# Norm's factor of the up product behind the down product, and state-space parameters prepared on VectorE

## The chip, the core and the metric

The kernel runs on one core of a Trainium2 chip. The core has TensorE (matmuls into PSUM), VectorE, ScalarE, GpSimd and SyncE, which issues most DMAs; each engine has its own queue and works in order, and semaphores order the engines against each other. The metric is the device time of one execution in microseconds (us), the median of several runs.

## The reference

One decode step of a hybrid model with two layers. 272 prompt tokens (16 meta tokens and 256) go as one sequence and 8 sample tokens as eight sequences of one, so 280 columns in all, in fp32. A layer is

```
h = x + 0.5 * swiglu(rmsnorm(x))          # ffn1: 1024 -> 2816 -> 1024
proj = rmsnorm(h) @ w_in                  # 1024 -> 2304
h = h + concat(s5, rwkv7, rglru) @ w_out  # three mixers on parts of proj
h = h + 0.5 * swiglu(rmsnorm(h))          # ffn2
swiglu(x) = (silu(x @ w_gate) * (x @ w_up)) @ w_down
```

`rmsnorm` divides each token by the root of its mean square: a factor for each column, once the activations lie with features on partitions and tokens in columns. The s5 mixer has parameters of its own that depend on weights alone: for 24 groups of 64 complex states a step `ab = exp(lambda * dt)`, an input matrix `bb = ((ab - 1) / lambda) * b`, and `c`. From them come, for four tokens at once, the powers of `ab` times `bb` and times `c`, and a table of cosines and sines.

## The kernel before

**Layout.** Activations `hres` are 8 tiles of 128 features by 280 tokens. Each fp32 operand of a large matmul is split in two fp32r parts, high and low (`xh`, `xl`; for weights `whi`, `wlo`), and a product takes three matmuls (`gemm`, L200 to L202). `wpiece` (L179) fetches a weight piece of 128 x 512, copies it to `whi` on ScalarE (L191) and takes the difference `wlo` on VectorE (L192: two inputs, both in SBUF). There are five buffers for the fetched piece, five for `whi`, four for `wlo`.

**The feed-forward block** (`ffn`, L313) runs four times. It takes the norm's factor `rs` (for each column, over the constant KR) once. Then 22 tiles f: gate and up product (24 matmuls each), the gate scaled by `rs` (L335), its tanh on ScalarE (L337), the up product scaled by `rs` (L339), their product (L340), times 1 + tanh (L341), and the split into `hh` on ScalarE (L342) and `hl` on VectorE (L343). Then 8 columns j of the down product, 66 matmuls each, added into `hres` with the factor 0.25 (L354), squared into the next norm's sum, and split for the next stage.

**The work beside it.** `beside` is a generator whose steps, up to a `yield`, are put in after chosen f and j (`slots`). In two blocks it is `s5_prepare` (ffn1 of layer 0, for that layer, and ffn2 of layer 0, for layer 1), with the slots `PREP`; in the other two (ffn1 of layer 1, ffn2 of layer 1) it writes the mixers' states, with the slots `STATE`. The scheduler that places the instructions keeps to the data and to these bounds from below, and may put a step's instructions later among those of the block.

**`s5_prepare`.** States and parameters are loaded, `lru_rates` and `exp_small` compute on columns of 2 or 12 (VectorE, many small instructions); `lam_times` (L455) multiplies the entering state by `ab`; sine and cosine on ScalarE (L517, L559); the rotation table `cs` from products of 17 coarse and 4 fine angles (L570 to L572), 408 columns at a time, on GpSimd. Then complex products, `ctimes` (L576): each takes four products on GpSimd (L583, L585) and two on VectorE (L584), first 12 pairs x 16 columns for `bb`, then for each T of three (4 pairs each) three more for the powers and four with 32 columns for `ct`. Between these, a T copies the powers into `bx` (L610, ScalarE), transposes `c` (L620) and `bx` (L630) on TensorE through the one bank of `psD`, copies them out (`c0` L624 on VectorE, `xbt` L631 on ScalarE), and multiplies them into `kin` (L638, L643, L646).

Of the kernel before, what the change touches and what calls it, by code (L numbers as in the profile page):

```python
# [19 lines left out]
KD = 8  # L20
# [54 lines left out]
def tile_hybrid_decode(ctx, tc, *args):  # L75
# [237 lines left out]
    def ffn(l, which, acc, cols, gnext, beside, slots):  # L313
# [6 lines left out]
        with tc.tile_pool(name="hid", bufs=1) as hp:  # L320
# [5 lines left out]
            for f in range(FT):  # L326
# [12 lines left out]
                V.scalar_tensor_tensor(u1, pu[:, :n], KR, rs, op0=MUL, op1=MUL)  # L339
                V.tensor_tensor(g1, g1, u1, op=MUL)  # L340
# [6 lines left out]
            for j in range(KD):  # L347
                js = slice(j * P, j * P + P)
                pd = psAB()
                for a, b in ((0, 8), (8, 16), (16, 22)):  # L350
                    w = wpiece(wd[:, a:b, js])
                    gemm(pd[:, :n], w, list(range(b - a)), hh[:, :, :n], hl[:, :, :n], list(range(a, b)), a == 0,
                         b == FT)
                V.scalar_tensor_tensor(hres[:, j, cols], pd[:, :n], 0.25, hres[:, j, cols], op0=MUL, op1=ADD)  # L354
                acc_sq(j, acc2, cols)
                if gnext is not None:
                    split_x(j, gnext, cols)
                if FT + j in slots:
                    next(job, None)
# [95 lines left out]
    def lam_times(out, lar, lai, hr, hi):  # L455

        sh = [P, NPA, ND]
        w = lambda: tmp("a", 6)[:, :NPA * ND].rearrange("p (a b) -> p a b", a=NPA)
        arb, aib = lar.unsqueeze(2).to_broadcast(sh), lai.unsqueeze(2).to_broadcast(sh)
        for r, x0, x1, op in ((0, hr, hi, SUB), (1, hi, hr, ADD)):  # L460
            a, b = w(), w()
            G.tensor_tensor(a, arb, x0, op=MUL)
            G.tensor_tensor(b, aib, x1, op=MUL)
            G.tensor_tensor(out[:, r], a, b, op=op)

    def s5_prepare(l, tp, e):
# [57 lines left out]
        for r, nm in enumerate(('re_in', 'im_in')):  # L524
            G.tensor_copy(e['h0'][:, r], e[nm][:, :, 0:ND])
# [36 lines left out]
        for p0 in (0, 6):  # L562
# [6 lines left out]
            for dst, x0, x1, y0, y1, op in ((co, ca, cb, sa, sb, SUB), (sn, sa, cb, ca, sb, ADD)):  # L569
                G.tensor_tensor(dst, x0, x1, op=MUL)  # L570
                G.tensor_tensor(t4, y0, y1, op=MUL)
                G.tensor_tensor(dst, dst, t4, op=op)  # L572
            yield
        e['cos'], e['sin'] = cs[:, 0], cs[:, 1]

        def ctimes(dst, ar, ai, x, shape, conj):  # L576

            n = shape[1] * shape[2]
            w = lambda: tmp("a", 6)[:, :n].rearrange("p (a b) -> p a b", a=shape[1])
            arb, aib = ar.unsqueeze(2).to_broadcast(shape), ai.unsqueeze(2).to_broadcast(shape)  # L580
            for r, op in ((0, ADD if conj else SUB), (1, SUB if conj else ADD)):
                p0, p1 = w(), w()
# [18 lines left out]
        c0 = tp.tile([P, 2, 4, 2, 16], F32, name="c0", tag="c0")  # L601
        G.memset(c0, 0.0)
        for T in range(3):
            ts = slice(4 * T, 4 * T + 4)
            sh = [P, 4, 16]
            b = bb[:, :, ts]
            for s in range(3, -1, -1):
                for q in range(2):
                    qs = slice(64 * q, 64 * q + 64)
                    S.activation(bx[qs, :, :, s, q], b[qs], AF.Copy)  # L610
                if s:
                    nb = tp.tile([P, 2, 4, 16], F32, name="nb", tag="nb", bufs=2)
                    ctimes(ri(nb), lar[:, ts], lai[:, ts], ri(b), sh, False)
                    b = nb
            yield
            pt = psD()
            for r in range(2):
                cd = tp.tile([P, 2, 64], F32, name="cd", tag="cd", bufs=2)
                G.tensor_copy(cd, cn[:, T, r].unsqueeze(1).to_broadcast([P, 2, 64]))
                PE.transpose(pt[:, r * P:r * P + P], cd.rearrange("p q n -> p (q n)"), ident)  # L620
            pv = pt[:, :2 * P].rearrange("p (r a q c) -> p r a q c", r=2, a=4, q=2)
            for q in range(2):
                qs = slice(64 * q, 64 * q + 64)
                V.tensor_copy(c0[qs, 0, :, q], pv[qs, 0, :, q])  # L624
                V.tensor_scalar(c0[qs, 1, :, q], pv[qs, 1, :, q], -1.0, None, op0=MUL)
# [10 lines left out]
            for a in range(4):  # L636
                for r in range(2):
                    PE.matmul(pv[:, a], bx[:, r, a].rearrange("p s q c -> p (s q c)"),  # L638
                              c0[:, r, a].rearrange("p q c -> p (q c)"), start=(r == 0), stop=(r == 1))
            dd = tp.tile([P, 4, 32], F32, name="dd", tag="dd")  # L640
            G.tensor_tensor(dd[lo], ident[lo, lo].unsqueeze(1).to_broadcast([32, 4, 32]),
                            d32[lo, ts].unsqueeze(2).to_broadcast([32, 4, 32]), op=MUL)
            V.tensor_tensor(dd[lo], pv[lo], dd[lo], op=ADD)  # L643
            for d in range(4):
                for j in range(4 - d):
                    S.activation(kin[32 * j:32 * j + 32, ts, j + d], (pv if d else dd)[96 - 32 * d:128 - 32 * d],  # L646
                                 AF.Copy)

            x = [c0[:, r].rearrange("p a q c -> p a (q c)") for r in range(2)]
# [883 lines left out]
    PREP = [f for f in range(FT) if f % 3 < 2] + list(range(FT, FT + KD))  # L1533
# [61 lines left out]
```

## Time and profile before

| | |
|---|---|
| median of 3 runs | 1278.68 us (1273.01 to 1279.05) |
| the profiled execution | 1279.83 us, span 1278.0 us |
| TensorE, VectorE | 1222.5 and 999.5 us busy |
| ScalarE, GpSimd | 690.2 and 348.9 us busy |
| mean granted clock of TensorE | 0.958 |

The span is the time from the first to the last instruction of the profiled execution. The first down column of the four blocks is evicted at 176.4, 598.2, 810.9 and 1208.0 us, the last at 239.9, 658.6, 869.1 and 1262.5; the mixers lie between the first and the second block and between the third and the fourth. Matmuls are pipelined, so a busy TensorE need not go at its full pace; the number of matmuls in a stretch says that. PE is TensorE, PEld its weight loads, DVE VectorE, ACT ScalarE, POOL GpSimd, SP SyncE.

### The profile page before, as it was taken

What the parts mean: (1) busy time and instruction counts of PE and PEld (TensorE: products, weight loads), DVE (VectorE), ACT (ScalarE), POOL (GpSimd) and SP (SyncE); (2) the same over time, 40 slices, a digit from 0 to 9 for tenths busy, and PEclk for the clock granted to TensorE, in tenths of its full rate; (3) what the DMA queues carried; (4) which work ended last, traced back from release to release, by engine and by line L of the source; (5) the groups of instructions that cost most, each with busy time, mean ns of one, the idle gap of its engine ahead of it and who ended that gap; (6) DMA issues with size and microseconds to landing.
All of it is one profiled execution on the core that took longest, in us unless ns stands there. A gap on an engine that the chain in (4) does not pass through costs nothing.

```text
span 1278.0 us, 29512 instructions
## 1 busy us (share of the span) xinstructions
PE 1222.5 (96%) x10744; PEld 1161.3 (91%) x10744; DVE 999.5 (78%) x2395; ACT 690.2 (54%) x1489; POOL 348.9 (27%) x619
## 2 busy tenths in 40 slices
PE   7999899999898999989999999999999989999997
PEld 6999899988776999989998999998888779999996
DVE  7999976679687799998667878756876778987854
ACT  4556565564355555656544555556633656555552
POOL 2104852033443210385207000001615332500000
PEclk9999999989897999989999999999995989999998
DMA  7665455524311756535578665654333028866662
GB/s 187 168 182 156 132 148 154 164 83 117 92 33 50 187 160 190 156 104 169 161 185 225 194 171 167 178 168 142 105 86 93 3 83 223 237 193 177 179 187 79
DMA packets 376911, 187.49 MB, mean 147 GB/s; under 512 B 45532, under 2 KB 375352, under 8 KB 376766
## 3 DMA queue, kind: packets, MB, share of 16 engines
q1 hardware_dynamic: 376430, 184.47, 52.0%
q8 instruction: 84, 1.38, 0.4%
q10 hardware_dynamic: 336, 1.15, 0.3%
q14 instruction: 61, 0.50, 0.1%
HBM read 181.31 MB, written 3.37 MB: 145 GB/s over the span
## 4 chain that ended last, share of the span: by engine, by line
PE 79%; DVE 11%; DMA 4%; issue 2%; ACT 2%; POOL 1%; SPq 0%; DVEq 0%; ACTq 0%; POOLq 0%
PE psa L202 11%; PE psa L201 11%; PE psa L200 10%; PE psc L201 6%; PE psc L202 6%; PE psc L200 6%; PE psb L202 6%; PE psb L200 6%; PE psb L201 6%; DVE wlo L192 3%; DMA stg<-in_ffn_w_gate_dram 2%; DMA stg<-in_ffn_w_up_dram 1%; PE psc L752 1%; PE psc L677 1%; PE psc L715 1%
## 5 line engine op out<-in xcount | busy, mean ns | idle before, releaser
L191 ACT ACTIVATE whi<-stg 128x512 fp32r<-128x512 f32 (+2 forms) x664 | 399.3, 608 | 354.4 <-PE psa L201 116.1
L192 DVE TENSOR_TENSOR wlo<-stg,whi 128x512 fp32r<-128x512 f32 (+2 forms) x640 | 445.8, 700 | 129.0 <-PE psa L202 35.3
L202 PE MATMUL psa<-xh,wlo 128*128 128x280 f32 (+1 forms) x930 | 275.7, 298 | 5.0 <-DVE wlo L192 4.5
L200 PE MATMUL psa<-xh,whi 128*128 128x280 f32 (+1 forms) x930 | 273.7, 295 | 2.8 <-DVE ts L1296 2.1
L201 PE MATMUL psa<-xl,whi 128*128 128x280 f32 (+1 forms) x930 | 272.9, 294 | 0.0
L202 PEld LDWEIGHTS psa<-xh,wlo 128*128 128x128 f32 x930 | 176.4, 190 | 10.4 <-DVE wlo L192 7.9
L200 PEld LDWEIGHTS psa<-xh,whi 128*128 128x128 f32 x930 | 177.5, 191 | 5.4 <-DVE ts L1296 2.3
L201 PEld LDWEIGHTS psa<-xl,whi 128*128 128x128 f32 x930 | 177.0, 190 | 1.8 <-issue 1.0
L202 PE MATMUL psc<-xh,wlo 128*128 128x280 f32 (+1 forms) x498 | 145.1, 292 | 1.8 <-DVE wlo L192 1.8
L200 PE MATMUL psc<-xh,whi 128*128 128x280 f32 (+1 forms) x498 | 145.2, 292 | 1.0 <-ACT xh L264 0.5
L201 PE MATMUL psc<-xl,whi 128*128 128x280 f32 (+1 forms) x498 | 144.8, 291 | 1.1 <-DVE xl L265 0.7
L202 PE MATMUL psb<-xh,wlo 128*128 128x280 f32 (+1 forms) x396 | 115.6, 292 | 1.3 <-DVE wlo L192 1.3
L200 PE MATMUL psb<-xh,whi 128*128 128x280 f32 (+1 forms) x396 | 115.8, 292 | 0.2 <-ACT whi L191 0.2
L201 PE MATMUL psb<-xl,whi 128*128 128x280 f32 (+1 forms) x396 | 115.3, 291 | 0.0
L202 PEld LDWEIGHTS psc<-xh,wlo 128*128 128x128 f32 x498 | 94.0, 189 | 2.8 <-DVE wlo L192 2.7
L200 PEld LDWEIGHTS psc<-xh,whi 128*128 128x128 f32 x498 | 94.0, 189 | 2.3 <-ACT xh L738 0.8
L201 PEld LDWEIGHTS psc<-xl,whi 128*128 128x128 f32 x498 | 94.0, 189 | 1.9 <-DVE xl L265 1.0
L202 PEld LDWEIGHTS psb<-xh,wlo 128*128 128x128 f32 x396 | 74.9, 189 | 2.2 <-DVE wlo L192 2.2
L200 PE MATMUL psb<-hh,whi 128*128 128x280 f32 (+1 forms) x264 | 76.7, 291 | 0.0
L200 PE MATMUL psa<-hh,whi 128*128 128x280 f32 (+1 forms) x264 | 76.6, 290 | 0.0
L202 PE MATMUL psb<-hh,wlo 128*128 128x280 f32 (+1 forms) x264 | 76.5, 290 | 0.0
L202 PE MATMUL psa<-hh,wlo 128*128 128x280 f32 (+1 forms) x264 | 76.5, 290 | 0.0
(618 smaller groups left out, 2743.3 us busy)
## 6 DMA issues: line engine op xcount, KB each, us to landing
stg<-in_ffn_w_gate_dram SPq DMA_DIRECT2D x176, 256.0 KB
stg<-in_ffn_w_up_dram SPq DMA_DIRECT2D x176, 256.0 KB
stg<-in_ffn_w_down_dram SPq DMA_DIRECT2D x160, 256.0 KB
stg<-in_w_in_dram SPq DMA_DIRECT2D x72, 256.0 KB
stg<-in_w_out_dram SPq DMA_DIRECT2D x32, 192.0 KB
bc<-ds SPq DMA_DIRECT2D x24, 192.0 KB
stg<-in_ffn_w_down_dram SPq DMA_DIRECT2D x32, 128.0 KB
bc<-ds SPq DMA_DIRECT2D x12, 256.0 KB
```

What stands on the lines that cost most here:

```text
L191: S.activation(hi[:, :kc], st[:, :kc], AF.Copy)
L192: (eng or V).tensor_tensor(lo[:, :kc], st[:, :kc], hi[:, :kc].bitcast(F32), op=SUB)
L200: PE.matmul(out, w[wk[i]][0], ah[:, k], start=(first and i == 0), stop=False)
L201: PE.matmul(out, w[wk[i]][0], al[:, k], start=False, stop=False)
L202: im = PE.matmul(out, w[wk[i]][1], ah[:, k], start=False, stop=(last and i == n - 1))
L677: PE.matmul(px[r][:, a], s5['xbt'][:, 4 * T + a, r], u4[:, 4 * T + a, 8:16 + NQ], start=True, stop=True)
L715: PE.matmul(py[32 * i:32 * i + 32, c0:c0 + n], w, x[:, o:NQ + ND], start=(m == 0), stop=(m == 2), skip_group_check=True, tile_position=(0, ...
L752: PE.matmul(pz[:, :NT], gw[k][:, j], z5[:, k, 0:NT], start=(k == 0), stop=(k == 2))
```

## The change

Two parts. In the block, the up product is no longer scaled by the norm's factor: L339 goes, the product with the scaled gate reads the up product in PSUM, and the factor `KR * rs` is multiplied to the down product, which takes one instruction more for each j. In the preparation, the rotation, `lam_times` and the complex products go to VectorE; a complex product takes one instruction for both parts of the first factor and four for the rest, and is made for all 12 pairs at once, so there are 8 of them and not 22; copies go from GpSimd and VectorE to ScalarE; the products of `ct` come after the three T; and the work is cut into more steps, with a slot after each f from 1 to 21 and two after each j.

```
-                V.scalar_tensor_tensor(u1, pu[:, :n], KR, rs, op0=MUL, op1=MUL)
-                V.tensor_tensor(g1, g1, u1, op=MUL)
+                V.tensor_tensor(g1, pu[:, :n], g1, op=MUL)
...
-                V.scalar_tensor_tensor(hres[:, j, cols], pd[:, :n], 0.25, hres[:, j, cols], op0=MUL, op1=ADD)
+                dh = tmp("f", NRK)[:, :n]
+                V.scalar_tensor_tensor(dh, pd[:, :n], 0.25 * KR, rs, op0=MUL, op1=MUL)
+                V.tensor_tensor(hres[:, j, cols], dh, hres[:, j, cols], op=ADD)
...
-                if FT + j in slots:
+                for _ in range(slots.count(FT + j)):
                     next(job, None)
...
-            G.tensor_tensor(a, arb, x0, op=MUL)
-            G.tensor_tensor(b, aib, x1, op=MUL)
-            G.tensor_tensor(out[:, r], a, b, op=op)
+            V.tensor_tensor(a, arb, x0, op=MUL)
+            V.tensor_tensor(b, aib, x1, op=MUL)
+            V.tensor_tensor(out[:, r], a, b, op=op)
...
-            G.tensor_copy(e['h0'][:, r], e[nm][:, :, 0:ND])
+            S.activation(e['h0'][:, r], e[nm][:, :, 0:ND], AF.Copy)
...
-                G.tensor_tensor(dst, x0, x1, op=MUL)
-                G.tensor_tensor(t4, y0, y1, op=MUL)
-                G.tensor_tensor(dst, dst, t4, op=op)
+                V.tensor_tensor(dst, x0, x1, op=MUL)
+                V.tensor_tensor(t4, y0, y1, op=MUL)
+                V.tensor_tensor(dst, dst, t4, op=op)
+                yield
+        e['cos'], e['sin'] = cs[:, 0], cs[:, 1]
+
+        def ctimes(dst, ar, ai, x, n, conj, tags):
+            na = x.shape[2]
+            sh = [P, na, n]
+            p0, p1 = (tp.tile([P, 2, na, n], F32, name="cp" + tg, tag=tg) for tg in tags)
+            aib = ai.unsqueeze(2).to_broadcast(sh)
+            V.tensor_tensor(p0, ar.unsqueeze(1).unsqueeze(3).to_broadcast([P, 2, na, n]), x, op=MUL)
+            for r in range(2):
+                V.tensor_tensor(p1[:, r], aib, x[:, 1 - r], op=MUL)
             yield
-        def ctimes(dst, ar, ai, x, shape, conj):
...
-                G.tensor_tensor(p0, arb, x[r], op=MUL)
-                V.tensor_tensor(p1, aib, x[1 - r], op=MUL)
-                G.tensor_tensor(dst[r], p0, p1, op=op)
...
+            V.tensor_tensor(dst[:, 0], p0[:, 0], p1[:, 0], op=ADD if conj else SUB)
+            V.tensor_tensor(dst[:, 1], p0[:, 1], p1[:, 1], op=SUB if conj else ADD)
...
-        ctimes(ri(bb), fr, fi, ri(bn), [P, NPA, 16], False)
+        yield from ctimes(bb, fr, fi, bn, 16, False, ("sta", "stre_in"))
...
+        dd = tp.tile([P, NPA, 32], F32, name="dd", tag="dd")
+        V.tensor_tensor(dd[lo], ident[lo, lo].unsqueeze(1).to_broadcast([32, NPA, 32]),
+                        d32[lo].unsqueeze(2).to_broadcast([32, NPA, 32]), op=MUL)
+        bl = [bb]
+        for s in range(3):
+            nb = tp.tile([P, 2, NPA, 16], F32, name=f"nb{s}", tag=("ang", "nb1", "nb2")[s])
+            yield from ctimes(nb, lar, lai, bl[-1], 16, False, ("sta", "stre_in"))
+            yield
+            bl.append(nb)
...
-                    S.activation(bx[qs, :, :, s, q], b[qs], AF.Copy)
+                    S.activation(bx[qs, :, :, s, q], bl[3 - s][qs, :, ts], AF.Copy)
...
-                G.tensor_copy(cd, cn[:, T, r].unsqueeze(1).to_broadcast([P, 2, 64]))
+                S.activation(cd, cn[:, T, r].unsqueeze(1).to_broadcast([P, 2, 64]), AF.Copy)
...
-                V.tensor_copy(c0[qs, 0, :, q], pv[qs, 0, :, q])
-                V.tensor_scalar(c0[qs, 1, :, q], pv[qs, 1, :, q], -1.0, None, op0=MUL)
+                for r in range(2):
+                    S.activation(c0[qs, r, ts, 16 * q:16 * q + 16], pv[qs, r, :, q], AF.Copy, scale=-1.0 if r else 1.0)
...
-            G.tensor_tensor(dd[lo], ident[lo, lo].unsqueeze(1).to_broadcast([32, 4, 32]),
-                            d32[lo, ts].unsqueeze(2).to_broadcast([32, 4, 32]), op=MUL)
-            V.tensor_tensor(dd[lo], pv[lo], dd[lo], op=ADD)
+            V.tensor_tensor(dd[lo, ts], pv[lo], dd[lo, ts], op=ADD)
...
-            for s in range(4):
-                y = [ct[:, r, ts, s] for r in range(2)]
-                ctimes(y, lar[:, ts], lai[:, ts], x, [P, 4, 32], True)
-                x = y
-                if s & 1:
-                    yield
+            yield
+
+        x = c0
+        for s in range(4):
+            y = ct[:, :, :, s]
+            yield from ctimes(y, lar, lai, x, 32, True, ("sta", "bx"))
+            yield
+            x = y
...
-    PREP = [f for f in range(FT) if f % 3 < 2] + list(range(FT, FT + KD))
+    PREP = list(range(1, FT)) + [FT + j for j in range(KD) for _ in range(2)]
```

## Rows read from the trace of the kernel before

**Rows 1.** The page, part 1: busy us, share of the span, instructions.
```profile
PE 1222.5 (96%) x10744; PEld 1161.3 (91%) x10744; DVE 999.5 (78%) x2395; ACT 690.2 (54%) x1489; POOL 348.9 (27%) x619
```

**Rows 2.** Table of windows: length; busy PE, PEld, DVE, ACT, POOL (x count); PEclk, DMA, GB/s.
```profile
168.00:240.00 72.00, 71.03 (x545) 70.80 (x544) 47.95 (x98) 41.90 (x92) 21.80 (x46) 0.98 0.54 155
455.00:592.00 137.00, 131.85 (x994) 130.16 (x994) 127.65 (x364) 79.79 (x167) 52.39 (x84) 0.98 0.52 150
...
680.00:804.00 124.00, 122.30 (x929) 119.76 (x928) 98.17 (x187) 62.61 (x121) 19.39 (x22) 1.00 0.68 190
804.00:870.00 66.00, 66.00 (x513) 66.00 (x512) 42.17 (x81) 34.27 (x63) 1.45 (x9) 1.00 0.60 173
```

**Rows 3.** Table of windows, finer, columns as in rows 2.
```profile
497.00:545.00 48.00, 48.00 (x376) 48.00 (x375) 46.55 (x174) 29.45 (x57) 14.21 (x27) 1.00 0.56 161
545.00:566.00 21.00, 17.31 (x107) 16.41 (x106) 18.75 (x28) 10.89 (x27) 19.21 (x26) 0.84 0.36 104
...
36.00:110.00 74.00, 73.61 (x573) 73.38 (x572) 70.77 (x246) 41.32 (x76) 8.74 (x16) 1.00 0.59 169
...
128.00:153.00 25.00, 21.57 (x161) 20.20 (x160) 23.04 (x39) 14.67 (x34) 22.27 (x26) 1.00 0.41 117
```

**Rows 4.** Timeline of VectorE, 545 to 563: start, us, engine, line, op, tiles, shapes.
```profile
545.50 0.43 DVE L339 SCALAR_TENSOR_TENSOR tf<-psb,nry 128x280 f32<-128x280 f32 x1
545.85 0.67 DVE L192 TENSOR_TENSOR wlo<-stg,whi 128x512 fp32r<-128x512 f32 x1
...
548.28 1.40 DVE L192 TENSOR_TENSOR wlo<-stg,whi 128x512 fp32r<-128x512 f32 x1
...
550.68 1.16 DVE L343 TENSOR_TENSOR hl<-tf,hh 128x280 fp32r<-128x280 f32 x1
```

**Rows 5.** Timeline of GpSimd, the same stretch; in brackets the idle time before.
```profile
546.09 1.21 POOL L570 TENSOR_TENSOR cs<-ang 128x408 f32<-128x408 f32 x1 [0.26 <-ACT ang L559]
```

**Rows 6.** Groups of VectorE, 455 to 592, then one of 804 to 870.
```profile
L192 DVE TENSOR_TENSOR wlo<-stg,whi 128x512 fp32r<-128x512 f32 x78 | 58.0, 749 | 3.6 <-ACT whi L191 3.5
L343 DVE TENSOR_TENSOR hl<-tf,hh 128x280 fp32r<-128x280 f32 x22 | 11.9, 542 | 0.7 <-ACT hh L342 0.7
L340 DVE TENSOR_TENSOR tf<-tf 128x280 f32<-128x280 f32 x20 | 10.9, 546 | 0.0
...
L339 DVE SCALAR_TENSOR_TENSOR tf<-psa,nry 128x280 f32<-128x280 f32 x9 | 4.0, 440 | 1.7 <-PE psa L202 1.7
...
L192 DVE TENSOR_TENSOR wlo<-stg,whi 128x512 fp32r<-128x512 f32 x39 | 26.7, 690 | 20.4 <-PE psa L202 8.5 <-PE psb L202 5.7 <-PE psc L202 4.6
```

**Rows 7.** Table of windows around the half clock, columns as in rows 2.
```profile
550.00:555.00 5.00, 2.91 (x21) 2.46 (x21) 5.00 (x7) 2.50 (x6) 5.00 (x6) 1.00 0.36 103
555.10:561.90 6.80, 6.80 (x32) 6.80 (x32) 6.30 (x9) 1.26 (x4) 6.66 (x10) 0.50 0.38 108
```

**Rows 8.** Waits, 455 to 592: waiter, releaser, us, times, longest.
```profile
PEld psd L620 <- POOL cs L572: 1.3, 1, 1.3
...
PE psd L638 <- ACT xbt L631: 0.8, 1, 0.8
```

**Rows 9.** Timeline of ScalarE at the last down column.
```profile
1262.58 2.95 ACT L1560 ACTIVATE hg<-hres,fgain 128x264 f32<-128x264 f32 x7 [6.25 <-PE psb L202]
...
1265.44 0.41 ACT L260 ACTIVATE tf<-hres 128x264 f32<-128x264 f32 x1
```

**Rows 10.** Instructions by line: ns least/median/most, first and last start.
```profile
L584 DVE TENSOR_TENSOR ta<-sms5n,bn x4: 345/346/346, 114.0 to 531.7; 128x192 f32<-128x192 f32 x4
...
L585 POOL TENSOR_TENSOR ct<-ta x48: 453/662/1051, 136.8 to 614.9; 128x128 f32<-128x128 f32 x48
...
L610 ACT ACTIVATE bx<-nb x36: 294/308/313, 118.6 to 601.4; 64x128 f32<-64x128 f32 x36
...
L631 ACT ACTIVATE xbt<-psd x12: 573/582/600, 135.6 to 613.0; 128x512 f32<-128x512 f32 x12
```

**Rows 11.** Waits, 36 to 168, columns as in rows 8.
```profile
PEld psd L630 <- issue: 1.9, 1, 1.9
```

More of the change, by code (lines that the diff above doesn't have):

```diff
@@ L569, in s5_prepare @@
             for dst, x0, x1, y0, y1, op in ((co, ca, cb, sa, sb, SUB), (sn, sa, cb, ca, sb, ADD)):
-                G.tensor_tensor(dst, x0, x1, op=MUL)
-                G.tensor_tensor(t4, y0, y1, op=MUL)
-                G.tensor_tensor(dst, dst, t4, op=op)
-            yield
-        e['cos'], e['sin'] = cs[:, 0], cs[:, 1]
-        def ctimes(dst, ar, ai, x, shape, conj):
[L578 to L582, printed above, removed]
-                G.tensor_tensor(p0, arb, x[r], op=MUL)
-                V.tensor_tensor(p1, aib, x[1 - r], op=MUL)
-                G.tensor_tensor(dst[r], p0, p1, op=op)
-        ri = lambda t: (t[:, 0], t[:, 1])
+                V.tensor_tensor(dst, x0, x1, op=MUL)
[11 more added lines that the diff above has]
+                V.tensor_tensor(p1[:, r], aib, x[:, 1 - r], op=MUL)
+            yield
+            V.tensor_tensor(dst[:, 0], p0[:, 0], p1[:, 0], op=ADD if conj else SUB)
+            V.tensor_tensor(dst[:, 1], p0[:, 1], p1[:, 1], op=SUB if conj else ADD)
         bb = tp.tile([P, 2, NPA, 16], F32, name="bb", tag="bb")
-        ctimes(ri(bb), fr, fi, ri(bn), [P, NPA, 16], False)
+        yield from ctimes(bb, fr, fi, bn, 16, False, ("sta", "stre_in"))
         lo = slice(96, 128)
@@ L600, in s5_prepare @@
         G.memset(bx, 0.0)
-        c0 = tp.tile([P, 2, 4, 2, 16], F32, name="c0", tag="c0")
+        c0 = tp.tile([P, 2, NPA, 32], F32, name="c0", tag="c0")
         G.memset(c0, 0.0)
+        dd = tp.tile([P, NPA, 32], F32, name="dd", tag="dd")
[7 more added lines that the diff above has]
+            bl.append(nb)
         for T in range(3):
             ts = slice(4 * T, 4 * T + 4)
-            sh = [P, 4, 16]
-            b = bb[:, :, ts]
-            for s in range(3, -1, -1):
+            for s in range(4):
                 for q in range(2):
                     qs = slice(64 * q, 64 * q + 64)
-                    S.activation(bx[qs, :, :, s, q], b[qs], AF.Copy)
[L611 to L614, printed above, removed]
+                    S.activation(bx[qs, :, :, s, q], bl[3 - s][qs, :, ts], AF.Copy)
             yield
@@ L637, in s5_prepare @@
                 for r in range(2):
-                    PE.matmul(pv[:, a], bx[:, r, a].rearrange("p s q c -> p (s q c)"),
-                              c0[:, r, a].rearrange("p q c -> p (q c)"), start=(r == 0), stop=(r == 1))
-            dd = tp.tile([P, 4, 32], F32, name="dd", tag="dd")
-            G.tensor_tensor(dd[lo], ident[lo, lo].unsqueeze(1).to_broadcast([32, 4, 32]),
-                            d32[lo, ts].unsqueeze(2).to_broadcast([32, 4, 32]), op=MUL)
-            V.tensor_tensor(dd[lo], pv[lo], dd[lo], op=ADD)
+                    PE.matmul(pv[:, a], bx[:, r, a].rearrange("p s q c -> p (s q c)"), c0[:, r, 4 * T + a],
+                              start=(r == 0), stop=(r == 1))
+            V.tensor_tensor(dd[lo, ts], pv[lo], dd[lo, ts], op=ADD)
             for d in range(4):
+                src = pv[96 - 32 * d:128 - 32 * d] if d else dd[lo, ts]
                 for j in range(4 - d):
-                    S.activation(kin[32 * j:32 * j + 32, ts, j + d], (pv if d else dd)[96 - 32 * d:128 - 32 * d],
-                                 AF.Copy)
-            x = [c0[:, r].rearrange("p a q c -> p a (q c)") for r in range(2)]
-            for s in range(4):
-                y = [ct[:, r, ts, s] for r in range(2)]
-                ctimes(y, lar[:, ts], lai[:, ts], x, [P, 4, 32], True)
-                x = y
-                if s & 1:
-                    yield
+                    S.activation(kin[32 * j:32 * j + 32, ts, j + d], src, AF.Copy)
+            yield
+        x = c0
+        for s in range(4):
+            y = ct[:, :, :, s]
+            yield from ctimes(y, lar, lai, x, 32, True, ("sta", "bx"))
+            yield
+            x = y
         e['xbt'], e['ct'], e['kin'] = xbt, ct, kin
```

## The prediction, made before the change was built

> **What bounds the kernel now.** I read the page first: TensorE is busy for 1222.5 of 1278.0 us, VectorE for 999.5, ScalarE for 690.2, GpSimd for 348.9 [rows 1]. So the matmuls set the time, and another engine matters only where it makes TensorE wait. The change touches the four feed-forward blocks, so I cut these into stretches by the table of windows. The cleanest is 804 to 870, the down columns of the third block, where no preparation runs: 513 matmuls in 66.0 us, 0.1287 us each, TensorE never idle [rows 2]. That is the pace to measure with; a tile f of 48 matmuls then takes 6.17 us and a down column of 66 takes 8.49.
>
> Length minus count times pace gives what a stretch loses. In the two blocks that prepare the state-space parameters the loss sits in few places [rows 3]. 36 to 110: 573 matmuls, 73.7 of 74 us, 0.3 lost. 497 to 545: 376, 48.4 of 48, nothing lost, although VectorE is 97% busy there (46.55 of 48). But 128 to 153: 161, 20.7 of 25, 4.3 lost; and 545 to 566: 107, 13.8 of 21, 7.2 lost. What sets these two apart is GpSimd, busy 22.27 of 25 and 19.21 of 21, against 8.74 of 74 in the first. The down columns of the first block lose another 1.9 (545 matmuls, 70.1 of 72 us) [rows 2]. Together 13.4 us.
>
> The timelines of 545 to 563 show how [rows 4, 5]. A weight split (wlo) takes 0.67 us at 545.85, begun in a pause of GpSimd, and 1.40 at 548.28, among GpSimd's products of the rotation (1.21 the first); hl takes 1.16 at 550.68. Over the whole f phase the splits average 749 ns against 690 where GpSimd rests, and hl and g1 u1 542 and 546, while an eviction of as many columns that reads PSUM takes 440 [rows 6]. So an instruction of VectorE with both inputs in SBUF is held up by one of GpSimd that reads SBUF. In the same stretch the granted clock was 0.50 (1.2 GHz) for 6.8 us, right behind 5 us in which TensorE was busy for only 2.91; there 32 matmuls took what 53 do at 2.4 GHz [rows 7]. The 7.2 us contain that.
>
> **The change, part by part.** *u1 leaves.* Per f one eviction of 440 ns goes; followers start 0.08 us before the end of the one ahead (545.50 + 0.43, next at 545.85 [rows 4]), so 0.36 us of VectorE per f, 7.9 per block. The product g1 u1, 546 ns with two SBUF inputs in preparation, becomes one that reads PSUM, 440 by the evictions [rows 6]. It now waits for the tanh before it frees the bank; behind it on VectorE stands the product with th, which waits for the same tanh, and the seven banks hold five gemms more, some 15 us, so I cost this at nothing; without that cover it would be about a pass over the tile, 0.44, per f. Its worth is only that VectorE gets ahead: in the state blocks (ffn2 of the last layer, ffn1 of it) TensorE is at its pace or waits for weights. 680 to 804 loses 4.5 us (929 matmuls, 119.5) [rows 2], so the bounds are 0 and 4.5 a block. VectorE is idle for 26 of these 124 us [rows 2], so it is not what they mostly lack; I take 0.5 in all.
>
> *One product more per down column*, 0.37 us net on VectorE, 8 per block, where it idles (42.17 busy of 66 [rows 2]). At the last column it stretches the chain into what follows: at most 0.45 x 4 = 1.8 us. At the very end ScalarE takes up the last column only at 1265.44: seven scaled copies, released by its matmuls at 1262.58, come first and last 2.95 [rows 9], and two passes of 0.45 fit into that. I take 0.3 in all.
>
> *GpSimd's products go to VectorE.* Per preparation GpSimd loses 12 rotation products, 88 of the complex products, 6 of lam_times, 6 copies cd, 2 copies h0 and 3 dd; memsets stay. VectorE loses 44 products L584, 3 dd adds stay, and 12 copies c0 go to ScalarE. It gains, by durations of its own undisturbed products (192 columns 346 ns [rows 10], 512 columns 670 [rows 4]: 1.01 ns a column and 0.15 fixed): rotation 12 x 408 columns, 0.56; four products with 16 columns a pair (384, then four of 192), 0.54 + 4 x 0.35; four with 32 (768, then four of 384), 0.93 + 4 x 0.54; lam_times 6 x 0.25 (96); dd 0.54 (384). Less 0.075 us of overlap each: 5.8 + 6.3 + 10.9 + 1.0 + 0.5 = 24.5 us per preparation. The f phase gets the 13.6 without the last four products and loses 7.9 (u1), some 9 of hold-ups (59 ns x 78 splits, 102 x 22, 106 x 20 [rows 6]) and about half of L584, 24 of at least 0.2: VectorE falls from 127.65 of 137 us to about 120. Since 97% did not starve TensorE in 497 to 545, this will not.
>
> *Where the steps now fall.* Slots are f 1 to 21 and two per column, 37; the generator yields 33 times (35 in layer 0). Layer 1: rotation f 6 to 9, products to f 16, T 0 from f 17, T 1 and T 2 into columns 0 and 1, the four ct products at columns 2 to 5; layer 0 one column later. A column with a ct product costs VectorE 42.17 / 7.77 columns = 5.43, + 0.37, + 2.73 = 8.53 of 8.49 us. The splits ahead (four tiles of 12 matmuls, 6 us) cover an excess that small. If the 0.075 of overlap is lost between dependent products, 9.0, or 0.5 over on four columns, 2.0 per preparation.
>
> The Trainium skill bears on that (VectorE: DVE Perf Modes, section The DRAIN you can't avoid): a next instruction does not start until the pipe is empty, so count instructions. The trace shows independent ones starting 0.08 us early [rows 4]; by the rule the column costs 9.0 and the sum below is 2 us worse.
>
> *ScalarE* gains 2 h0, 6 cd and 12 c0 copies, by its small copies (308 ns [rows 10]) 6.2 us per preparation. The c0 copies wait there for TensorE's transposes, with weight splits whi queued behind them, on which TensorE waits in turn. The one DMA in the moved steps, d32, goes to SP's queue among the weights as before: nothing. In columns 0 and 1 (0 to 2 in layer 0) two thirds of a T land on it: T costs 24 x 0.308 + 2 x 0.582 = 8.6 [rows 10], the column 34.27 / 7.77 = 4.4 [rows 2], together 10.1 of 8.49 plus a T's own 26 matmuls. Bounds for both engines: 0, all inside the lookahead, and 2.0 + 3.2 per preparation. I take 1.0, near nothing, because whi has five tiles ahead: 2.0 in all.
>
> **The sum.** Of the 13.4 us, TensorE's own waits for the preparation stay: 1.9 for c0 [rows 11] and 0.8 for xbt [rows 8], which I allow in both blocks; the wait for cd behind GpSimd's rotation (1.3 [rows 8]) goes. So 13.4 - 3.5 = 9.9 to gain. -9.9 - 0.5 + 0.3 + 2.0 = -8.1. The profiled execution took 1279.83, which gives 1271.7; it stands 1.15 above the median of the runs, 1278.68, so 1270.6.
>
> **Rivals.** *VectorE only trades.* The rotation and the products come as chains in which each waits for the one before, on an engine already 93% busy; splits wait behind bursts of 2.75 us instead of behind GpSimd, and the columns give back up to 10.4. For it: the f phase is tighter than any other stretch. Against: 497 to 545. With half the 9.9 gained and the columns' 2.0 to 5 lost it leaves up to 3 us: 1276 to 1279. Chance 0.26.
>
> *More than this.* Without the gap before it the half clock goes too, TensorE's waits for c0 shrink (nothing else queues ahead on ScalarE), and the state blocks give 2 to 3: the whole 13.4 + 2.5 - 0.3 = 15.6, so 1278.7 - 15.6 = 1263. Against: xbt's round trip through one PSUM bank is unchanged. Chance 0.17.
>
> *The tail comes late.* Steps are a lower bound: before, the sine that starts the rotation is ready only at 546 [rows 5], though the rotation's slot, f 7, is due near 455 + 7 x 6.17 = 498. Now three T and then four ct products queue behind it in one chain. Before, the last product ended at 615 [rows 10], some 45 us ahead of its block's end (592, the end of the f stretch, + 8 x 8.49). If the chain runs past the last column, the factor of the mixer's norm queues behind it on VectorE, 11 us per preparation: 1270.6 + 22 = 1292.6. It ends slower than no change by 0.5% once more than 8.1 + 6.4 = 14.5 us of the two tails stand behind the last column, 2.6 of four products each. Chance 0.07.
>
> **How the numbers follow.** Forecast 0.50, for 1266 to 1275. 0.5%, 6.4 us, is about what a measurement here can tell from none: faster is below 1272.3. Some four fifths of the forecast, and all of "more", lie there: 0.41 + 0.17 = 0.58. Same: 0.09 + 0.26 = 0.35. Slower: 0.07. The range runs from "more" (1262) to just above no change (1279.5).
>
> **What would show it.** Right: in f 10 to 17 of both blocks, TensorE at 0.129 us a matmul, splits at 680 to 690 ns, no half clock, GpSimd with memsets alone; last ct product before the last column. Wrong: TensorE waiting on wlo or whi in the columns, splits late behind products of 0.95 us, or the first stretch of the mixers later against the last column.

## The result and the profile after

The changed kernel takes 1258.14 us (median of 4 runs, 1257.17 to 1266.57), the kernel before beside it 1277.43: a ratio of 0.987 [0.983, 0.991]. The forecast was 1270.6, its range 1262 to 1279.5. So the sign was right, but the time lies 4 us below the range: the gain is 19 us by the medians, some 16 by the ratio, where 8 were forecast.

Each kernel was profiled twice. The table cuts the spans where the last column of a block is added into `hres` and where the last mixer's output is; it gives lengths in us.

| stretch | before | before, again | changed | changed, again | means differ by |
|---|---|---|---|---|---|
| first block (prepares layer 0) | 240.4 | 239.2 | 234.3 | 235.5 | -4.9 |
| mixers of layer 0 | 193.9 | 194.2 | 192.2 | 189.6 | -3.2 |
| second block (prepares layer 1) | 224.9 | 224.8 | 216.5 | 216.8 | -8.2 |
| third block (states) | 210.5 | 211.3 | 209.3 | 209.7 | -1.4 |
| mixers of layer 1 | 195.5 | 195.4 | 194.9 | 193.5 | -1.3 |
| fourth block (states) | 197.9 | 197.7 | 196.5 | 197.3 | -0.9 |
| from there to the end | 15.1 | 13.5 | 13.0 | 13.1 | -1.3 |
| span | 1278.0 | 1276.2 | 1256.8 | 1255.6 | -20.9 |

The two blocks that prepare give 13.1 of the 20.9. The page of the changed kernel shows GpSimd down by 134.5 us [rows 1] and VectorE, which took the work over, busy for 27.6 us less than before:

```profile
PE 1211.6 (96%) x10744; PEld 1154.9 (92%) x10744; DVE 971.9 (77%) x2345; ACT 698.0 (56%) x1529; POOL 214.4 (17%) x385
```

Windows of the changed kernel, in the order first block, second block, third block (length; busy PE, PEld, DVE, ACT, POOL with counts; PEclk, DMA, GB/s):

```profile
128.00:153.00 25.00, 25.00 (x196) 25.00 (x196) 23.31 (x56) 15.22 (x34) 0.00 (x0) 1.00 0.63 180
166.00:238.00 72.00, 71.88 (x567) 71.65 (x565) 50.58 (x98) 49.12 (x121) 1.95 (x11) 1.00 0.53 155
447.20:572.00 124.80, 124.11 (x968) 123.89 (x968) 112.52 (x347) 76.23 (x154) 3.42 (x4) 1.00 0.58 167
545.00:566.00 21.00, 21.00 (x166) 21.00 (x166) 16.60 (x39) 14.11 (x35) 0.00 (x0) 1.00 0.54 157
592.00:640.00 48.00, 48.00 (x378) 48.00 (x377) 38.60 (x74) 29.10 (x66) 0.00 (x0) 1.00 0.55 159
663.90:787.90 124.00, 122.07 (x938) 120.76 (x937) 96.02 (x174) 64.05 (x121) 17.49 (x22) 1.00 0.68 189
787.90:853.90 66.00, 66.00 (x513) 66.00 (x512) 43.77 (x86) 34.05 (x64) 2.05 (x14) 1.00 0.60 173
```

The two stretches that lost most are at the full pace: 128 to 153 holds 196 matmuls where there were 161, and 545 to 566 holds 166 where there were 107 [rows 3]; the granted clock is 1.00 (2.4 GHz) in all of them. TensorE's weight loads waited in the two blocks for this and no more (first 36 to 234, then 440 to 643; us, times, longest):

```profile
PEld psa L202 <- DVE wlo L192: 1.1, 2, 0.8
PEld psd L490 <- POOL sta L415: 0.3, 1, 0.3
...
PEld psb L202 <- DVE wlo L192: 0.9, 1, 0.9
```

Nothing waits on `psd` for the steps of a T any more; before it was 1.9 for `c0` [rows 11], and `cd` and `xbt` in the second block [rows 8]. VectorE's groups in the f tiles of the second block, 447 to 572 (count, busy us, mean ns, idle before and its releaser):

```profile
L192 DVE TENSOR_TENSOR wlo<-stg,whi 128x512 fp32r<-128x512 f32 x78 | 52.7, 685 | 1.7 <-ACT xbt L638 1.3 <-PE psb L202 0.3
L343 DVE TENSOR_TENSOR hl<-tf,hh 128x280 fp32r<-128x280 f32 x21 | 9.3, 442 | 1.1 <-ACT hh L342 1.1
...
L340 DVE TENSOR_TENSOR tf<-psa,tf 128x280 f32<-128x280 f32 x9 | 4.0, 444 | 1.8 <-PE psa L202 1.8
```

The splits are back from 749 to 685 ns, `hl` from 542 to 442, and the product with `pu` takes 444 where it took 546 [rows 6].

### The profile page after: what moved, and what is told of

Read it like the earlier page. It is cut to its first block, busy times and chain, and to the rows that moved or that the text cites. A ratio compares the mean times of both kernels' runs of the same rounds, so it can differ in the third digit from the quotient of the medians.

```text
span 1256.8 us, 29154 instructions
## 1 busy us (share of the span) xinstructions
PE 1211.6 (96%) x10744; PEld 1154.9 (92%) x10744; DVE 971.9 (77%) x2345; ACT 698.0 (56%) x1529; POOL 214.4 (17%) x385
## 4 chain that ended last, share of the span: by engine, by line
PE 83%; DVE 8%; DMA 4%; POOL 2%; issue 2%; ACT 1%; SPq 1%; DVEq 0%; ACTq 0%; POOLq 0%
PE psa L202 11%; PE psa L201 11%; PE psa L200 11%; PE psc L201 6%; PE psc L202 6%; PE psc L200 6%; PE psb L202 6%; PE psb L201 6%; PE psb L200 6%; PE psc L756 1%; DVE wlo L192 1%; PE psc L719 1%; PE psc L681 1%; PE psb L901 1%; DMA bc<-ds 1%
## 5 line engine op out<-in xcount | busy, mean ns | idle before, releaser
L192 DVE TENSOR_TENSOR wlo<-stg,whi 128x512 fp32r<-128x512 f32 (+2 forms) x640 | 432.6, 682 | 129.2 <-ACT whi L191 29.9
L201 PE MATMUL psb<-hl,whi 128*128 128x280 f32 (+1 forms) x264 | 76.7, 291 | 0.0
L201 PE MATMUL psa<-hl,whi 128*128 128x280 f32 (+1 forms) x264 | 76.6, 290 | 0.0
```

The source lines that it names most:

```text
L192: (eng or V).tensor_tensor(lo[:, :kc], st[:, :kc], hi[:, :kc].bitcast(F32), op=SUB)
L201: PE.matmul(out, w[wk[i]][0], al[:, k], start=False, stop=False)
```

## The experiments

**Theory.** GpSimd, reading SBUF, holds up those instructions of VectorE that have two inputs in SBUF, and this made TensorE wait. **First rival:** VectorE's load, which falls with u1 and with fewer, larger products, is what counts. **Second rival:** the new steps and slots are. The first five kernels separate these. Below, "the two blocks" are those that prepare, their lengths added: 465.3 and 464.0 us before, 450.8 and 452.3 changed.

**Norm's factor alone** (`norm_only`). The kernel before, with only the feed-forward block changed:

```
-                V.scalar_tensor_tensor(u1, pu[:, :n], KR, rs, op0=MUL, op1=MUL)
-                V.tensor_tensor(g1, g1, u1, op=MUL)
+                V.tensor_tensor(g1, pu[:, :n], g1, op=MUL)
...
+                V.scalar_tensor_tensor(dh, pd[:, :n], 0.25 * KR, rs, op0=MUL, op1=MUL)
+                V.tensor_tensor(hres[:, j, cols], dh, hres[:, j, cols], op=ADD)
```

> The kernel before with the norm's factor alone moved behind the down product; the preparation stays as it was, on GpSimd and VectorE. Hold-up theory (GpSimd's reads of SBUF hold up VectorE's instructions with two SBUF inputs, and that is what costs TensorE): little, 1274 to 1277 us against 1277.4. Rival, VectorE's load (what costs is the sum of VectorE's work in the f phase, and the eviction that goes, 7.9 us a block, relieves it): half of the gain or more, 1268 or less.

Measured: 1269.70 us, ratio 0.994 [0.991, 0.997]: 8 us by the ratio, well above the theory's 1274 to 1277 and near the half of the gain that the first rival had asked for. Taken by itself this run speaks for that rival. The two blocks take 460.0, and what they gain lies in the second (220.5; the first takes 239.5). Windows of the second block's f tiles:

```profile
455.00:592.00 137.00, 134.04 (x1035) 132.25 (x1034) 127.51 (x357) 84.00 (x174) 57.95 (x101) 1.00 0.55 157
...
520.00:545.00 25.00, 24.04 (x186) 23.29 (x185) 24.86 (x49) 17.63 (x38) 22.05 (x32) 1.00 0.48 138
```

VectorE is still full (24.86 of 25 us) where GpSimd is busy (22.05), and TensorE still loses there (186 matmuls are 23.9 us at its pace). But the pause that the half clock followed [rows 7] is gone: PEclk is 1.00. As I read it, 0.36 us less per f gives VectorE some lead before it gets there; the lead itself was not measured. This half is worth more than the forecast gave it as long as GpSimd still reads.

**Preparation alone** (`prep_only`). The changed kernel with norm's factor put back where it was (the edit above, reversed).

> The changed kernel with the norm's factor back on the up product; the preparation on VectorE in more steps. Hold-up theory: most of the gain, 1260 to 1264. Rival, VectorE's load: less than half, 1268 or more, since VectorE has the products and the eviction besides.

Measured: 1270.12 us, ratio 0.992 [0.989, 0.995]. The total misses the theory's 1260 to 1264 and lies where the first rival had put it, but the two blocks are at 454.7, 10 us under those of before. What they gain is lost again in the mixers of layer 0: 202.1 us there at a mean granted clock of 0.84, where the changed kernel's second profile has 189.6 at 0.93. The row of this kernel, then that of the changed one:

```profile
236.10:438.20 202.10, 189.76 (x2058) 163.71 (x2057) 150.86 (x389) 108.01 (x275) 71.29 (x137) 0.84 0.32 89
```

```profile
235.50:425.10 189.60, 174.99 (x2067) 150.82 (x2066) 147.35 (x383) 105.72 (x270) 70.77 (x130) 0.93 0.34 94
```

By the clock records that is 64.8 against 27.3 us at 1.2 GHz (twice 0.16 of 202.1 is 64.7), so 12.5 us of length for 37.5. The other profiles, of before and of every experiment, lie within 1.1 us of that line, a third of a us for each at half clock; only `old_slots`, below, has a tail of its own in this stretch. Long mixers are the rule for this kernel and no accident of one profile: seven of its nine runs took 1268.7 to 1272.9 us at a mean granted clock of 0.949 to 0.956, the other two 1258.7 and 1262.3 at 0.964 and 0.962. Why it meets more of such stretches is open. So the totals hold something that the change in the blocks does not explain, and the lengths of the blocks are the better witness.

**Only the engine changed** (`engines_only`). The kernel before, its steps, slots and sizes, with the products that GpSimd computed on VectorE (norm's factor unchanged, `c0` still on VectorE, `cd` still on GpSimd):

```
-            G.tensor_tensor(a, arb, x0, op=MUL)
+            V.tensor_tensor(a, arb, x0, op=MUL)
...
-                G.tensor_tensor(dst, x0, x1, op=MUL)
+                V.tensor_tensor(dst, x0, x1, op=MUL)
...
-                G.tensor_tensor(p0, arb, x[r], op=MUL)
+                V.tensor_tensor(p0, arb, x[r], op=MUL)
```

> The kernel before with GpSimd's products of the rotation, lam_times, the complex products and dd put on VectorE, and nothing else: 22 complex products of six instructions each, the old slots, the old factor, copies where they were. Hold-up theory: the gain of prep_only less what some 19 us of extra instructions per preparation cost on VectorE, 1263 to 1270. Rival, the merging (fewer, longer instructions and more steps make the gain): none, 1276 or more.

Measured: 1261.66 us, ratio 0.987 [0.984, 0.990], the same as the whole change and a little better than the theory had asked for; the two blocks 449.5. Windows of this kernel:

```profile
545.00:566.00 21.00, 21.00 (x166) 20.98 (x165) 21.00 (x57) 13.19 (x28) 0.00 (x0) 1.00 0.57 164
128.00:153.00 25.00, 24.36 (x193) 24.13 (x191) 24.60 (x68) 17.49 (x33) 0.00 (x0) 1.00 0.55 159
```

The first row decides between the theory and the first rival. VectorE is busy for 21.00 of 21 us, more than the 18.75 of before [rows 3], with 57 instructions and not 28, and TensorE runs at its pace (166 matmuls, not 107). Over the two blocks, from end to end, VectorE is busy for 398 us here, for 390 in the kernel before, with its held-up instructions, and for 373 in the changed one. The most work goes with blocks as short as the changed kernel's. The waits of its weight loads, first 36 to 240 and then 440 to 640:

```profile
PEld psa L200 <- ACT whi L191: 0.9, 1, 0.9
PEld psa L202 <- DVE wlo L192: 0.8, 1, 0.8
...
PEld psc L202 <- DVE wlo L192: 0.5, 1, 0.5
```

No wait for `c0`, `cd` or `xbt` is left, though none of the copies has changed its engine.

**Engine and norm's factor** (`engines_and_norm`, `changed_again`). The two edits above together, without the new steps and slots, beside the changed kernel on the same chip.

> engines_only and the norm's factor behind the down product together: no merged products, old slots. If merging and more steps are worth something beside the engine: slower than the changed kernel, 1261 or more. If the gain is the hold-up's alone, and stalls of 2 to 3 us a block are the floor: like the changed kernel, 1256 to 1260. If the gains of norm_only and engines_only add: 1251 to 1254.

> The changed kernel once more, beside the three others on the same chip, for comparison with them: 1256 to 1260.

Measured: 1261.55 us, ratio 0.988 [0.984, 0.991], and 1261.14, ratio 0.987 [0.984, 0.990]; the two blocks 450.9 and 452.3. Both lie just above the 1256 to 1260 expected, and cannot be told apart. With GpSimd's products gone, norm's factor adds nothing that is clear of the scatter, nor do larger products in more steps: the second rival falls as a source of the gain.

**The rotation back on GpSimd** (`rotation_back`). The changed kernel with 12 products of 408 columns per preparation on GpSimd again:

```
-                V.tensor_tensor(dst, x0, x1, op=MUL)
-                V.tensor_tensor(t4, y0, y1, op=MUL)
-                V.tensor_tensor(dst, dst, t4, op=op)
+                G.tensor_tensor(dst, x0, x1, op=MUL)
+                G.tensor_tensor(t4, y0, y1, op=MUL)
+                G.tensor_tensor(dst, dst, t4, op=op)
```

> The changed kernel with the 12 products of the rotation per preparation back on GpSimd, the rest on VectorE. Hold-up theory: splits of 1.4 to 1.5 us return around them, and 3 to 8 us are lost against the changed kernel's 1258.1: 1261 to 1266. Rival, VectorE's load: VectorE has 6 us less per preparation, so no loss, 1256 to 1259.

Measured: 1263.66 us, ratio 0.989 [0.985, 0.992]; the two blocks 454.6. VectorE's groups in 100 to 166 of this kernel:

```profile
L192 DVE TENSOR_TENSOR wlo<-stg,whi 128x512 fp32r<-128x512 f32 x42 | 32.5, 779 | 4.5 <-PE psb L202 2.5 <-ACT whi L191 1.7 <-issue 0.2
...
L343 DVE TENSOR_TENSOR hl<-tf,hh 128x280 fp32r<-128x280 f32 x11 | 5.7, 515 | 0.6 <-ACT hh L342 0.6
L340 DVE TENSOR_TENSOR tf<-psa,tf 128x280 f32<-128x280 f32 x5 | 2.2, 442 | 1.1 <-PE psa L202 1.1
```

Twelve products on GpSimd lift the mean of 42 splits by some 90 ns and that of `hl` by 70; the product that reads PSUM stays at 442. The rotation is a part of the hold-ups, and by the blocks 2 to 4 us of the time (the changed kernel's own two profiles differ by 1.5); the totals, ratio 0.989 against 0.987, do not separate the two kernels.

**Reading and only writing** (`gpsimd_reads`, `gpsimd_writes`). The changed kernel, and GpSimd given work that nothing waits for, after each f from 4 on in the two blocks: five products that read SBUF, or in their place ten memsets (`G.memset(dmp, 0.0)`), both behind a copy of one column on ScalarE that paces them.

```
+                if f >= 4 and slots is PREP:
+                    S.activation(dmp[:, 0:1], u1[:, 0:1], AF.Copy)
+                    for _ in range(5):
+                        G.tensor_tensor(dmp, cmask[:, 0:160], cmask[:, 100:260], op=MUL)
```

> The changed kernel, and in the two preparing blocks five GpSimd products of 128x160 after each f from 4 on, which read a constant in SBUF and whose result nobody uses: some 2.5 us of GpSimd per f, about what it did before the change. Hold-up theory: splits rise from 686 to 720 ns or more, TensorE's stalls in these blocks go from 2.4 and 3.1 back towards 9 and 10, and the time to 1264 to 1270. Rival, the chain (what cost was that the preparation's own chain went to and fro between GpSimd and the others, and TensorE waited for its results): no change against the changed kernel, 1256 to 1260.

> The same with ten memsets of 128x160 on GpSimd in place of the five products: as long busy, but reading nothing. If only GpSimd's reads hold VectorE up: splits at 685 to 695 ns and 1256 to 1260. If any work of GpSimd does: as gpsimd_reads.

Measured, on the chip of the changed kernel's 1261.14 us: with reads 1293.20, ratio 1.013 [1.009, 1.017]; with memsets 1267.82, ratio 0.992 [0.988, 0.995]. The two blocks are 479.0 with reads, 26.7 more than 452.3, and 450.2 with memsets, no more at all. Both totals miss what was expected: with reads the time is far above 1264 to 1270, with memsets it is above 1256 to 1260. The memsets' 6.7 us lie behind the blocks, mostly in the mixers of layer 0 (198.6 us, 51.2 of them at half clock). Reads (a window, GpSimd's group, VectorE's groups, 40 to 166):

```profile
40.00:166.00 126.00, 117.38 (x870) 112.66 (x869) 122.70 (x333) 65.25 (x137) 60.36 (x80) 1.00 0.51 147
...
L348 POOL TENSOR_TENSOR dmp<-cmask 128x160 f32<-128x160 f32 x76 | 57.6, 758 | 53.2 <-ACT dmp L346 48.6
...
L192 DVE TENSOR_TENSOR wlo<-stg,whi 128x512 fp32r<-128x512 f32 x71 | 51.9, 742 | 0.2
L344 DVE TENSOR_TENSOR hl<-tf,hh 128x280 fp32r<-128x280 f32 x18 | 9.9, 552 | 0.3 <-ACT hh L343 0.2
...
L341 DVE TENSOR_TENSOR tf<-psa,tf 128x280 f32<-128x280 f32 x7 | 3.1, 436 | 0.0
```

Memsets, the same views:

```profile
40.00:166.00 126.00, 125.28 (x973) 124.82 (x972) 114.54 (x352) 75.62 (x164) 45.86 (x184) 1.00 0.58 167
...
L348 POOL MEMSET dmp<- 128x160 f32 x180 | 42.5, 236 | 60.0 <-ACT dmp L346 50.7
...
L192 DVE TENSOR_TENSOR wlo<-stg,whi 128x512 fp32r<-128x512 f32 x80 | 54.3, 688 | 4.7 <-PE psb L202 2.6 <-ACT whi L191 1.3 <-issue 0.6
```

With reads the splits are at 742 ns, `hl` at 552, and VectorE has hardly an idle moment left (122.70 of 126 us), yet only 870 matmuls fit; with memsets 973 do, and a split takes 688, though GpSimd is busy for 45.86 us. (973 - 870) x 0.1287 = 13.3 us, which is the block's loss. The product that reads PSUM takes 436 ns under the reads, as undisturbed. This is the theory's mechanism, made at will, and without the chain that the expectation names as a rival: nothing waits for these products. The Trainium skill has the rule (SBUF — State Buffer, section Who interferes with whom): a VectorE instruction with two SBUF inputs contends with a GpSimd instruction that reads SBUF, and not with one that only writes it. The runs agree in both halves: 742 against 688 ns.

**The slots of before** (`old_slots`). The changed kernel with 23 slots in place of 37.

```
-    PREP = list(range(1, FT)) + [FT + j for j in range(KD) for _ in range(2)]
+    PREP = [f for f in range(FT) if f % 3 < 2] + list(range(FT, FT + KD))
```

> The changed kernel with the slots of before (23 in place of 37), so that 10 to 12 of the preparation's steps, the four last products among them, are handed out only behind the last down column. Hold-up theory: nothing in the f stretches changes, TensorE keeps its pace there. Rival that the late tail costs: the four products (some 2.7 us of VectorE each) and the rest of the last T stand ahead of the mixer's first work, up to 11 us per preparation, 1270 to 1283 us in all. If the scheduler finds room for them beside the mixer's matmuls, it is within 3 us of the changed kernel (1255 to 1264).

Measured: 1299.25 us, ratio 1.015 [1.011, 1.019]: 38 us over the changed kernel, more than the rival asked for. The mixers of layer 0 take 227.4 us, and the block behind the second preparation 222.6. TensorE behind the first block's last column, and a window of the same stretch:

```profile
244.88 0.69 PE L627 MATMUL psd<-ident,cd 128*128 128x128 f32 x2 [5.27 <-ACT kin L651]
246.32 1.12 PE L637 MATMUL psd<-ident,bx 128*128 128x128 f32 x4 [0.76 <-ACT c L632]
248.12 1.11 PE L637 MATMUL psd<-ident,bx 128*128 128x128 f32 x4 [0.69 <-ACT xbt L638]
249.93 3.62 PE L645 MATMUL psd<-c,bx 128*128 128x32 f32 x16 [0.69 <-ACT xbt L638]
256.93 1.18 PE L278 MATMUL psd<-ones,acc 128*128 128x1 f32 x6 [3.38 <-ACT kin L651]
...
238.00:254.00 16.00, 8.15 (x41) 6.70 (x40) 2.33 (x5) 7.67 (x26) 0.00 (x0) 0.63 0.12 34
```

In these first 16 us it is not VectorE's products that cost (2.33 busy), which alone I had priced, but the chain of the last T through the one bank of `psD`: transposes, ScalarE's copies, `kin`, and behind them in the same bank the sums of the mixer's norm (L278), which come only at 256.93. TensorE pauses, and the clock goes to half behind it (0.63 mean). The products have their turn next, as the rival had it: they fill VectorE from 253.92 to 265.17, the norm's small steps stand between them, and TensorE waits for these:

```profile
254.00:264.00 10.00, 1.18 (x6) 1.08 (x6) 9.63 (x22) 2.76 (x10) 0.00 (x0) 0.50 0.00 1
...
265.99 1.74 PE L285 MATMUL psd<-ident,nrm 128*128 128x128 f32 x6 [7.88 <-DVE nrm L169]
```

The norm's steps from L280 to L169 take 7.7 us there and 3.7 in the changed kernel. So the new slots gain nothing of themselves, but the change needs them: its order puts all of T before four further products.

**State blocks too** (`state_blocks`). The changed kernel with the five products of GpSimd in the mixers' state steps on VectorE:

```
-                G.tensor_tensor(sd, sd, bc[:, 0], op=MUL)
+                V.tensor_tensor(sd, sd, bc[:, 0], op=MUL)
...
-                G.tensor_tensor(sd, sd, bc[:, 2], op=ADD)
+                V.tensor_tensor(sd, sd, bc[:, 2], op=ADD)
```

> The changed kernel, and in the two blocks that write the mixers' states GpSimd's five products per step on VectorE too (some 27 us of GpSimd per block, after which hardly anything but memsets is left to GpSimd there). Hold-up theory: the mean split falls from 712 to about 690 ns, but VectorE idles for a fifth of these blocks, and TensorE stalls there for only 3.8 us of each, mostly for weights, so the time stays within 3 us: 1255 to 1264. If hold-ups set the pace there as they did beside the preparation, the blocks gain 2 to 3 us each: 1252 to 1256. If VectorE cannot take the added products (about 20 us a block), the blocks lose more than 3 us.

Measured: 1258.12 us, ratio 0.986 [0.983, 0.989], not to be told from the changed kernel's. The third block takes 207.1 us, the fourth 197.4. Groups of this kernel and then of the changed one, 660 to 785:

```profile
L192 DVE TENSOR_TENSOR wlo<-stg,whi 128x512 fp32r<-128x512 f32 x81 | 55.1, 685 | 10.9 <-ACT whi L191 5.7 <-issue 2.8 <-ACT tf L337 1.0
```

```profile
L192 DVE TENSOR_TENSOR wlo<-stg,whi 128x512 fp32r<-128x512 f32 x79 | 55.5, 706 | 11.0 <-issue 6.2 <-ACT whi L191 2.6 <-ACT tf L337 0.6
```

The hold-ups go here as well, and the total does not show it. VectorE waits for 11 us of this stretch before its splits in both kernels; one with time to spare can take a hold-up without passing it on. That it passes on nothing is not shown: the third block is 2.2 to 2.6 us shorter than in the changed kernel's two profiles, but `prep_only`, with these products on GpSimd, has 207.2 there.

**The kernel before, once more** (`before_again`), for the scatter of what the change leaves alone.

> The kernel before once more, for the scatter of what the change does not touch. If TensorE's stretches at half clock fall differently from run to run in the mixers and at the end, the mixers' lengths (193.9 and 195.5 us in the first profile) move with them, by about a third of a microsecond for each microsecond at half clock, while the two blocks that prepare keep 240 and 225 us within 1.5. If the stretches belong to this kernel, the mixers come out within 1 us of the first profile, and the end (15.1 us from the last column on, with 3.4 us at half clock in it 2 us behind that column) does too.

Measured: 1277.96 us. Its windows answer to [rows 3]:

```profile
128.00:153.00 25.00, 21.58 (x161) 20.21 (x160) 22.96 (x38) 14.65 (x35) 22.27 (x26) 1.00 0.42 122
545.00:566.00 21.00, 15.66 (x105) 14.75 (x104) 18.13 (x27) 10.90 (x27) 19.53 (x26) 0.90 0.35 100
```

The losses repeat to two matmuls, and so do the mixers (within 0.3 us). The end does not: 13.5 us, without the 3.4 us at half clock that the first profile has there.

## Why the prediction was wrong in size

**Where TensorE loses time, and why: right.** Stretches, pace and hold-ups are as told. The result shows every sign asked for in f 10 to 17: 0.127 to 0.128 us a matmul in the two windows (the short ones of the preparation among them), splits at 685, no half clock, GpSimd at 0.00. The last product of `ct` starts at 227.40 and 628.46, ahead of the last columns' additions at 233.88 and 642.59:

```profile
227.40 0.55 DVE L590 TENSOR_TENSOR ct<-cpsta,cpbx 128x384 f32<-128x384 f32 x1
...
628.46 0.55 DVE L590 TENSOR_TENSOR ct<-cpsta,cpbx 128x384 f32<-128x384 f32 x1
```

**The step that failed: "TensorE's own waits for the preparation stay", 3.5 us.** They went, in both blocks. `engines_only` shows that this needs no other engine for `c0` or `cd`: with GpSimd's products gone, the waits are gone. In `norm_only`, with these products still on GpSimd, no weight load in the two blocks waits for `c0` or `cd` either. I had taken them for the preparation's own round trips through PSUM. For `c0` the trace of before shows otherwise. The row of [rows 11] names no releaser, but TensorE's own wait does, and VectorE's timeline tells what the copies stood behind:

```profile
PE psd L630 <- DVE c L625: 1.7, 1, 1.7
...
129.71 0.85 DVE L343 TENSOR_TENSOR hl<-tf,hh 128x280 fp32r<-128x280 f32 x1 [1.10 <-ACT hh L342]
130.48 0.21 DVE L624 COPY c<-psd 64x64 f32<-64x64 f32 x1
...
130.98 0.22 DVE L625 TENSOR_SCALAR c<-psd 64x64 f32<-64x64 f32 x1
```

The transposes that these copies take up had run at 67.5, so this was no round trip: the copies stood in VectorE's queue behind an `hl` for which VectorE had waited 1.10 us, and which then took 0.85 us where an undisturbed one takes 0.44. About 0.4 of the 1.7 us is a hold-up, and the rest the place in a queue. How much of the waits for `xbt` is either was not separated.

**The second term: 2.0 us for loaded columns.** Nothing of it appeared. 592 to 640, with the four products in it, holds 378 matmuls in 48.00 us without an idle moment, and no weight load waits for ScalarE. The overlap of 0.08 us is kept where other work stands between dependent steps. VectorE in the changed kernel:

```profile
541.17 0.35 DVE L589 TENSOR_TENSOR bb<-cpsta,cpstre_in 128x192 f32<-128x192 f32 x1
541.44 0.35 DVE L590 TENSOR_TENSOR bb<-cpsta,cpstre_in 128x192 f32<-128x192 f32 x1
541.71 0.44 DVE L341 SCALAR_TENSOR_TENSOR tf<-tf 128x280 f32<-128x280 f32 x1
542.07 0.68 DVE L192 TENSOR_TENSOR wlo<-stg,whi 128x512 fp32r<-128x512 f32 x1
```

The rule of the Trainium skill that I weighed (VectorE: DVE Perf Modes, section The DRAIN you can't avoid) would have made it 2 us worse; these starts go against it as I put it. The section itself goes on that a next instruction that is not held starts earlier, and the trace agrees with that: 0.08 us before the end of the one ahead.

With these two terms at their measured size, none, the two blocks come to -13.4, and -13.1 was measured. That alone makes the forecast about 1265, which is inside the range; the rest of the miss is below.

**Norm's factor: 0.5 us in the state blocks.** Alone it took 0.5 and 1.1 us off them, on top of `engines_only` 0.4 and 0.5, but `prep_only`, without it, has 405.7 for both blocks and the changed kernel 405.8 and 407.0. Two profiles of one kernel differ by up to 0.8 in one block, so these runs neither confirm the 0.5 nor refute it. In the blocks that prepare, the forecast did not see that this edit is worth 4 us in the second one as long as GpSimd reads, and nothing clear of the scatter once it doesn't. The added product per column costs nothing: 513 matmuls in 66.00 us, as before [rows 2].

**VectorE at "about 120".** 112.5 us for 968 matmuls, by count 115.5 for the 994 of before, some 4 us less than I took. I had priced the hold-ups of three groups. The product with 1 + tanh (L341), which also has two inputs in SBUF, is a fourth: 519 ns before against 441, 1.6 us for its 21; the rest of the 4 us was not taken apart. Its row before (455 to 592), then in the changed kernel (447 to 572):

```profile
L341 DVE SCALAR_TENSOR_TENSOR tf<-tf 128x280 f32<-128x280 f32 x21 | 10.9, 519 | 0.1
```

```profile
L341 DVE SCALAR_TENSOR_TENSOR tf<-tf 128x280 f32<-128x280 f32 x21 | 9.3, 441 | 0.0
```

**What no term covered: about 6 us in the mixers and at the end.** By the lengths, the mixers of layer 0 follow their time at half clock in every kernel but `old_slots`, and the first profile of before had a half-clock stretch at its end that the second had not. The clocks of all runs on record say how much of the 6 us this is. Take off a third of a us for each at half clock (an estimate, from the mixers of layer 0). Then the changed kernel's two series average 1228.8 and 1228.6 us, and the kernel before, beside the experiments, 1243.5 to 1244.2: some 15 us of gain, about the two blocks' 13.1 and the state blocks' 2.3. What is left is time at half clock, 94 and 98 us against 101 to 105, worth 1 to 4 us. The first median also came out low: six more runs of the changed kernel had 1261.14. Whether the change shifts these stretches for good is open; `prep_only` and `gpsimd_writes`, with long mixers behind good blocks, say that a kernel may meet more or fewer of them for reasons that none of these runs shows.

**The rivals.** "More than this" (1263, chance 0.17) comes nearest, and two of its three parts happened: the half clock gone and the waits for `c0` gone. The third, 2 to 3 us in the state blocks, is there in the table (2.3) but not clear of the scatter. It deserved more: a wait in a disturbed stretch should not have been booked as permanent. "VectorE only trades" falls with `engines_only`, where VectorE is busy without a break for 21 us and TensorE keeps its pace. "The tail comes late" did not occur, but `old_slots` shows that it was one line away, at 38 us and not 22.

## What to carry to other kernels

Where a stretch is disturbed, the small waits in it may go with the disturbance, or with the order in a queue, until a run shows otherwise: book them as gain and loss in two separate cases, not as a constant. Look beside an engine's busy time at the mean duration of one instruction in the stretch against an undisturbed one; a full VectorE fed TensorE at its pace, a slightly idler one with held-up splits did not. Work on GpSimd that reads SBUF is not free beside VectorE instructions with two SBUF inputs where VectorE has no time to spare; and when steps are reordered, count the slots, for what is left over runs alone.

## What the hardware showed beyond expectation

GpSimd's memsets (180 of 236 ns in 126 us) left the splits at 688 ns, while 76 products that read SBUF lifted them to 742 and cost the block 13.3 us, twice and more what the added nanoseconds of its 71 splits and 18 `hl` make up ((742 - 687) x 71 + (552 - 444) x 18 = 5.8 us; 687 and 444 are the changed kernel's); the rest was not taken apart. In the mixers of layer 0, 37.5 us more at 1.2 GHz came with 12.5 us more of length; which of the two brings the other no run here separates.
